# Where the even sums of down-projection pairs 2 to 11 are kept: weight-operand ring, or the two raw-weight tiles

## The chip, the cores and the metric

One core of one Trainium2 chip runs the whole program. The time is the device time of one execution in microseconds (us); of several executions the median is given. Engines are named as in the profile: PE multiplies matrices, PEld loads its weights, DVE and ACT are the vector and the scalar engine, POOL and SP are used here for moving data and for issuing DMAs.

## What is computed

Two layers of a small decoder, for 1024 prompt tokens and 8 sample tokens together (1032 columns, model width 1024). Layer 0 mixes tokens by a gated linear recurrence, layer 1 by windowed attention; each is followed by the same MLP, and only the MLP matters here:

```
def sq_relu_mlp(x, w_up, w_down):
    return jnp.square(jax.nn.relu(x @ w_up)) @ w_down
...
yp = yp + sq_relu_mlp(rms_norm(yp, norm_mlp_g[layer]), mlp_w_up[layer], mlp_w_down[layer])
```

`w_up` is 1024 x 4096 and `w_down` 4096 x 1024.

## The kernel before, in words

Activations lie transposed, features on the 128 partitions and 1032 columns. A matrix product is made in three passes: each operand is split into a rounded high part (ACT copy) and the low rest (DVE subtract), and PE adds high x high, high x low and low x high.

The two MLP projections are made in **pairs** of row blocks by a scheme of seven products in place of eight (2x2 blocks with sums and differences of blocks). `PROG` lists the products: 16 "up" pairs, then 20 "dn" (down) pairs, each with its products in the order 1, 2, 6, 7, 5, 4, 3. The first 14 of the 16 hidden pairs are handled so, in five chunks (`CHUNKS`: 3, 3, 3, 3 and 2 hidden pairs); four down pairs belong to each chunk, so down pairs 0 to 15 have 3 hidden pairs each and pairs 16 to 19 have 2. A product of the first kind is 3 x 3 x 2 = 18 matmuls of 258 columns, a pair 126. The rest of the hidden features follows at the end as an ordinary product (`down_steps`, matmuls of line 226).

Each down pair gathers two tiles of sums, the even one `he` and the odd one `ho` (128 x 1032). In order of the products: ACT copies product 1 from PSUM to `he` (line 633), DVE adds product 2 (635), ACT copies product 6 to `ho` and product 7 to the other half of `ho`, DVE adds to `ho` (637, 641), ACT copies product 3's sum to the other half of `he`. The four copies wait for PE, and PE waits for them: the third product goes on adding into the PSUM tile that the copy of the first one reads, the fifth into what the copy of the third reads. Then POOL adds `ho` and `he` to sums in DRAM by an accumulating DMA (line 652, "spill" in the profile); pairs 16 to 19 add from DRAM instead (654).

Tiles come from pools of fixed numbers of buffers, and an instruction that writes a new tile waits until the buffer's last user is done (for a stored tile: until its DMA has landed):

- `wp`, tag W, 12 buffers ("ring of weight operands"): the seven split weight operands `op` of a pair (lines 395 and 396: high and low in one tile), the two tiles `ws` of sums of weight blocks (line 497), and in down pairs 2 to 11 also `he`.
- `ap`, tag A, 33 buffers: activations, loaded hidden sums `tl` (line 542, POOL's DMA queue; split on ACT 401 and DVE 402), `ho`, and `he` of the other pairs.
- `rp`, tag R, 2 buffers: raw weights of the up pairs (fetched by SP, line 159), and the last four raw weight tiles of a layer (`last_weights`, line 604).
- tag Q, 4 buffers: raw weights of the down pairs, two tiles each (SP, line 159).

A list scheduler sets each engine's order of instructions; it knows the buffers, so a change of pools changes the order. Each engine, and SP's and POOL's DMA issuing too, then works strictly down its list: an instruction that waits holds up all that stand behind it. Operands are built some products ahead: after each product `pw.look(n)` lets the plan build up to a place in the next pair, as far as buffers are free.

Of the kernel before, what the change touches and what calls it, by code (L numbers as in the profile page):

```python
# [10 lines left out]
F32 = mybir.dt.float32  # L11
# [5 lines left out]
P = 128  # L17
D = 1024
M8 = D // P
SEQ = 1024  # L20
NS = 8
T = SEQ + NS
# [5 lines left out]
CHUNKS = [range(0, 3), range(3, 6), range(6, 9), range(9, 12), range(12, 14)]  # L28
# [31 lines left out]
def trunk(ctx: ExitStack, tc: tile.TileContext, I, O):  # L60
    nc = tc.nc
    pe, act, dve, pool, sp = nc.tensor, nc.scalar, nc.vector, nc.gpsimd, nc.sync

    cp = ctx.enter_context(tc.tile_pool(name="cp", bufs=1))
    ap = ctx.enter_context(tc.tile_pool(name="ap", bufs=33))
    wp = ctx.enter_context(tc.tile_pool(name="wp", bufs=12))
    rp = ctx.enter_context(tc.tile_pool(name="rp", bufs=2))
# [13 lines left out]
    def swap_small(name, bufs):  # L81
        open_small.close()
        small["pool"] = open_small.enter_context(tc.tile_pool(name=name, bufs=bufs, reuse_waits="tile"))
# [5 lines left out]
    def nm(s):  # L89
        cnt[0] += 1  # L90
        return f"{s}{cnt[0]}"

    def A(s="a"):
        return ap.tile([P, T], F32, tag="A", name=nm(s))
# [4 lines left out]
    def S(s="s"):  # L99
        return small["pool"].tile([P, CH], F32, tag="S", name=nm(s))  # L100
# [12 lines left out]
    def DB(tag):  # L113
        return psum["pool"].tile([P, 1024], F32, tag="D" + tag, bufs=2 if tag == "G" else 1, name=nm("bD"))

    def quarters(x):
        return x.rearrange("p (b c) -> p b c", b=2)

    def inner(d):
        return quarters(d)[:, :, 0:QT]  # L120
# [22 lines left out]
    def VV(n):  # L143
        o, w = VEC[n]
        return vec[:, o:o + w]
# [4 lines left out]
    raws = []  # L150

    def fetch(n):
        while len(raws) < min(n, len(units)):
            name, _, src, _ = units[len(raws)]
            if name[:2] == "dn":
                raws.append(small["pool"].tile([P, RQ], F32, tag="Q", name=nm("raw")))
            else:
                raws.append(rp.tile([P, D], F32, tag="R", name=nm("raw")))
            sp.dma_start(raws[-1][:, 0:src.shape[1]], src)

    def split_unit(raw, alloc, eng, parts=1):
# [209 lines left out]
    def factors(stat, ps):  # L371
        ssq, out = stat
        ssq.total(ps[:, :CH])
        rstd_m2(ps[:, :CH], out)
# [25 lines left out]
    def op_at(hi, lo):  # L400
        act.copy(r_(hi), lo)  # L401
        dve.tensor_tensor(r_(lo), lo, hi, ALU.subtract)  # L402
        return hi, lo
# [120 lines left out]
    def product(d, first, w, xs):  # L524
        n = len(xs)
        for j, (xh, xl) in enumerate(xs):
            for a, (wt, xt) in enumerate(((w[0], xh), (w[0], xl), (w[1], xh))):
                for b in range(2):
                    pe.matmul(d[:, 512 * b:512 * b + QT], lhsT=r_(wt[:, j * P:j * P + P]),  # L529
                              rhs=r_(xt[:, QT * b:QT * b + QT]),  # L530
                              start=first and j == 0 and a == 0, stop=j == n - 1 and a == 2,
                              skip_group_check=not first)
# [36 lines left out]
    def sums_of(e, o, to):  # L569
        t = small["pool"].tile([P, T], F32, tag="U", name=nm("ts"))  # L570

        def put(k, x):
            act.dma_start(to[:, k * HALF:k * HALF + x.shape[1]], x)

        put(2, o)
        yield
        dve.tensor_tensor(t[:, H0], e[:, H1], e[:, H0], ALU.subtract)
        dve.tensor_tensor(e[:, H1], o[:, H1], e[:, H1], ALU.subtract)
        dve.tensor_tensor(t[:, H1], o[:, H1], t[:, H0], ALU.subtract)
        yield  # L580
        put(0, e)
        put(4, t)
        dve.tensor_tensor(o[:, H0], o[:, H0], t[:, H1], ALU.subtract)
        yield
        put(6, o[:, H0])
# [3 lines left out]
    def mlp_products(layer, tok, pw, r, spill, acc, gnext, after):  # L589
        ahead = Ahead(layer)  # L590
        hs, raw = [], []
# [2 lines left out]
        xs[:] = [None] * M8  # L594
        st, stores = {}, []

        def last_tile(k):
            lo, hi = A("hdl"), A("hdh")
            pool.dma_start(lo, hid[layer][k])
            return hi, lo  # L600

        def last_weights(j):
            t = rp.tile([P, D], F32, tag="R", name=nm("raw"))
            sp.dma_start(t, I["w_dn"][layer][8 * len(CHUNKS) + j])
            return t

        for n, (kind, q, i) in enumerate(PROG):
            up = kind == "up"
            w, x = BY[i]
            if up and n in (1, 3, 5, 7, 9):  # L610
                tok.make(("B22", "T3", "T2", "T1", "T4")[n // 2])
            if n == 6:
                factors(rs.pop("late"), DB("Y"))
                swap_small(f"u{layer}", 3)
            if (kind, q, i) == ("up", NSP, 5):
                swap_small(f"q{layer}", 4)
            wt = pw.take(n)
            first = up and q < 2
            if i == 1:
                st[q] = {2: DB("X" if first and q == 1 else "Y"), "g": DB("G"),  # L620
                         "e": (W if not up and q in range(2, 12) else A)("he"), "o": A("ho")}
            z = st[q]
            alone = i in (1, 2, 7) or (i == 3 and first)
            if alone and i in (3, 7):
                z[i] = DB("Y" if first and q == 0 else "X")
            d = z["g"] if i in (1, 5, 6) else z[7] if i == 4 else z.get(i, z["g"])
            product(d, alone, wt, (tok if up else ahead).ops[x] if up else ahead.ops[q // 4][x])
            e, o, g = z["e"], z["o"], inner(z["g"])
            e0, e1, o0, o1 = [quarters(t[:, h]) for t in (e, o) for h in (H0, H1)]
            if i in (1, 6, 7, 3):  # L630
                t, f = {1: (e0, g), 6: (o0, g), 7: (o1, inner(d)), 3: (e1, inner(d))}[i]
                with tc.high_priority():
                    last["copy"] = act.copy(t, f).ins  # L633
            if i == 2:
                dve.tensor_tensor(e0, inner(d), e0, ALU.add)
            elif i == 5:
                dve.tensor_tensor(o1, g, o1, ALU.add)  # L637
                if 3 in z:
                    dve.tensor_tensor(e1, g, e1, ALU.add)
            elif i == 4:  # L640
                dve.tensor_tensor(o0, inner(d), o0, ALU.add)  # L641
            ready = {4: "o", 3: "" if alone else "e", 5: "e" if 3 in z else ""}.get(i, "")
            if ready and up:
                t = z[ready]
                dve.scalar_tensor_tensor(t, t, 0.0, r, ALU.min, ALU.mult)  # L645
                act.activation(t, t, AF.Square)  # L646
                if q >= NSP:
                    act.dma_start(hid[layer][2 * (q - NSP) + (ready == "o")], t)
            elif ready:
                m, t = 2 * (q % 4) + (ready == "o"), z[ready]  # L650
                if q < 4 * len(CHUNKS) - 4:
                    pool.dma_start(acc[m], t, accum_op=ALU.add)  # L652
                else:
                    pool.dma_start(t, acc[m], accum_op=ALU.add)
                    xs[m] = t
            if i == (4 if 3 in z else 3):
                if up and q < NSP:
                    stores.append(sums_of(e, o, hsum[layer][q]))
                del st[q]
            pw.look(n)  # L660
            for g in stores:
                next(g, None)
            if up and q == NPAIR - 1:
                k = ORDER.index(i)
                ahead.fetch(0, 3 * (k + 1), n)
                ahead.split(n)
            elif not up:
                c, k = q // 4, 7 * (q % 4) + ORDER.index(i)
                ahead.split(n)
                if c + 1 < len(CHUNKS):  # L670
                    ahead.fetch(c + 1, 11 * k // 20 if k <= 20 else 11 + 3 * (k - 20) // 2, n)
                k += 28 * (c - 3)
                if k in LAST["tile"]:
                    raw.append(last_tile(LAST["tile"].index(k)))
                if k in LAST["weights"]:
                    wraw.append(last_weights(LAST["weights"].index(k)))
                with tc.issue_after(last["copy"]):
                    if k in LAST["split tile"]:
                        hs.append(op_at(*raw.pop(0)))
                    if k in LAST["split weights"]:  # L680
                        ws.append(split_unit(wraw.pop(0), W, dve))
# [413 lines left out]


    sp8 = cp.tile([P, M8], F32, name="sp8")
    nsp8 = cp.tile([P, M8], F32, name="nsp8")
    lam = VV("lam")
    with_e = S("e")[:, :M8]  # L1100
    with_z = S("z")[:, :M8]
    act.activation(with_e, lam, AF.Abs)
# [276 lines left out]
```

## Time and profile before

| | us |
|---|---|
| median of 3 runs (2040.08 to 2043.04) | 2040.84 |
| the profiled execution's own time | 2038.14 |
| its span, first to last instruction | 2036.3 |
| PE busy | 2003.5 (98%) |
| DVE, ACT, POOL busy | 1413.2, 1051.9, 352.5 |
| mean granted TensorE clock | 0.996 |
| first to last matmul of the down pairs, layer 0 | 674 to 960 |
| the same, layer 1 | 1700 to 1988 |

The span is the profiler's; the time around it (1.8 us) belongs to start and end. PE is busy nearly throughout, so what counts is where PE stands still, and for whom. "Idle before" in the profile is the time an engine stood before an instruction, and the arrow names what ended it.

### The profile page before, as it was taken

Reading aid. Unit: us, or ns where it says so; the run is one execution under the profiler, and the core shown is the slowest. Engines: PE = TensorE matmul, PEld = TensorE weight load, DVE = VectorE, ACT = ScalarE, POOL = GpSimd, SP = SyncE. Lnnn points to the kernel's source line nnn. Section 1 sums busy time; section 2 is a strip of 40 time slices with the busy share of each in tenths; the row PEclk is TensorE's granted clock in tenths of the full one; section 3 lists DMA queues with packets and bytes.
Section 4 is the critical chain, followed back from the end, with each engine's and each line's share of the span. In section 5 each row is a group of like instructions: output and inputs, shape, how many; then the busy total and the mean of one; then the engine's idle time right before and its main releaser. Section 6 shows DMA issues by size and latency. Waiting matters only on the chain.

```text
span 2036.3 us, 38639 instructions
## 1 busy us (share of the span) xinstructions
PE 2003.5 (98%) x15106; PEld 1957.5 (96%) x15106; DVE 1413.2 (69%) x2673; ACT 1051.9 (52%) x2090; POOL 352.5 (17%) x562
## 2 busy tenths in 40 slices
PE   9989999999999999999999999999999999999999
PEld 8989999999999999999988887999999999999999
DVE  8887537876766766766846777569766666777663
ACT  6475635544343655555457776555434435555450
POOL 2541100000001223221003434100000003323220
PEclk9989999999999999999999999999999999999999
DMA  5112142344445777877443435612543447887683
GB/s 175 52 32 55 53 167 84 105 154 143 148 139 197 233 216 213 230 178 179 129 108 84 106 99 175 234 63 83 171 157 130 162 167 235 218 224 219 166 200 105
DMA packets 121047, 304.87 MB, mean 150 GB/s; under 512 B 20888, under 2 KB 53152, under 8 KB 120864
## 3 DMA queue, kind: packets, MB, share of 16 engines
q1 hardware_dynamic: 64864, 135.41, 21.6%
q0 software_dynamic: 28352, 98.30, 19.0%
q10 hardware_dynamic: 27648, 68.70, 9.3%
q8 instruction: 118, 1.93, 0.4%
q14 instruction: 65, 0.53, 0.1%
HBM read 176.22 MB, written 113.44 MB: 142 GB/s over the span
## 4 chain that ended last, share of the span: by engine, by line
PE 84%; issue 4%; DMA 3%; DVE 2%; ACT 2%; POOL 1%; SPq 0%; POOLq 0%; ACTq 0%
PE bD L529 54%; PE bP L226 11%; PE bS L226 6%; PE bP L768 4%; PE bT L226 3%; PE bO L889 2%; PE bS L848 1%; PE bT L868 1%; PE bN L714 1%; DMA spill<-ho 1%; DMA spill<-he 1%; DMA tl<-hsum 1%; PE bS L796 1%; POOL t L1170 0%; POOL tl L542 0%
## 5 line engine op out<-in xcount | busy, mean ns | idle before, releaser
L529 PE MATMUL bD<-op,op 128*128 128x258 f32 x5376 | 648.5, 283 | 0.0
L529 PEld LDWEIGHTS bD<-op,op 128*128 128x128 f32 x5376 | 647.9, 189 | 0.3
L529 PE MATMUL bD<-tl,op 128*128 128x258 f32 x4704 | 570.1, 284 | 4.4 <-ACT ho L633 4.1
L529 PEld LDWEIGHTS bD<-tl,op 128*128 128x128 f32 x4704 | 568.5, 190 | 5.8 <-ACT ho L633 4.5
L542 POOL DMA_DIRECT2D tl<-hsum x196 | 115.5, 674 | 900.2 <-ACT ho L633 421.6
L396 DVE TENSOR_TENSOR op<-ws,op 128x512 fp32r<-128x512 f32 (+2 forms) x288 | 168.5, 598 | 84.2 <-ACT op L395 84.2
L633 ACT COPY ho<-bD 128x516 f32<-128x516 f32 x144 | 85.1, 591 | 226.8 <-PE bD L529 226.8
L402 DVE TENSOR_TENSOR tl<-tl 128x516 fp32r<-128x516 f32 x196 | 130.6, 692 | 93.5 <-ACT tl L401 89.8
L395 ACT CAST op<-ws 128x512 fp32r<-128x512 f32 (+2 forms) x288 | 153.4, 550 | 42.0 <-DVE op L396 23.4
L633 ACT COPY he<-bD 128x516 f32<-128x516 f32 x144 | 84.0, 583 | 167.6 <-PE bD L529 167.6
L396 DVE TENSOR_TENSOR op<-raw,op 128x512 fp32r<-128x512 f32 (+2 forms) x216 | 124.1, 597 | 62.6 <-ACT op L395 62.6
L395 ACT CAST op<-raw 128x512 fp32r<-128x512 f32 (+2 forms) x216 | 114.1, 549 | 43.6 <-PE bD L529 20.3
L401 ACT CAST tl<-tl 128x516 fp32r<-128x516 f32 x196 | 115.3, 627 | 3.5 <-DMA tl<-hsum 3.5
L646 ACT ACTIVATE ho<-ho 128x1032 f32<-128x1032 f32 x32 | 34.2, 1070 | 107.5 <-DVE ho L645 107.5
L166 DVE TENSOR_TENSOR wl<-raw,wh 128x1024 fp32r<-128x1024 f32 (+1 forms) x57 | 68.1, 1201 | 25.1 <-ACT wh L165 20.3
L641 DVE TENSOR_TENSOR ho<-bD,ho 128x516 f32<-128x516 f32 x72 | 49.9, 694 | 43.3 <-PE bD L529 43.3
L859 POOL TENSOR_SCALAR se<-se,den 128x256 f32<-128x256 f32 (+1 forms) x128 | 66.4, 524 | 76.3 <-DVE den L857 74.3
L165 ACT CAST wh<-raw 128x1024 fp32r<-128x1024 f32 (+1 forms) x60 | 58.6, 988 | 37.1 <-DMA raw<-w_in 15.3
L652 POOL DMA_DIRECT2D spill<-ho x32 | 28.7, 896 | 257.2 <-DVE ho L641 245.9
L852 DVE CUSTOM_DVE_ANT_0 se<-bS,bias,nsink 128x256 f32<-128x256 f32 (+1 forms) x128 | 56.4, 461 | 21.6 <-PE bS L848 16.8
L855 ACT ACTIVATE se<-se,den 128x257 f32<-128x257 f32 (+1 forms) x128 | 63.0, 496 | 14.8 <-DVE den L852 13.2
L637 DVE TENSOR_TENSOR ho<-bD,ho 128x516 f32<-128x516 f32 x72 | 49.8, 691 | 20.2 <-PE bD L529 13.1
(299 smaller groups left out, 3743.6 us busy)
## 6 DMA issues: line engine op xcount, KB each, us to landing
tl<-hsum POOLq DMA_DIRECT2D x196, 258.0 KB, 7.2
raw<-w_up SPq DMA_DIRECT2D x64, 512.0 KB, 3.7
raw<-w_dn SPq DMA_DIRECT2D x64, 384.0 KB, 6.6
spill<-ho POOLq DMA_DIRECT2D x32, 516.0 KB, 5.6
spill<-he POOLq DMA_DIRECT2D x32, 516.0 KB, 7.2
hsum<-ho ACTq DMA_DIRECT2D x28, 516.0 KB, 3.7
hsum<-he ACTq DMA_DIRECT2D x28, 516.0 KB, 2.7
hsum<-ts ACTq DMA_DIRECT2D x28, 516.0 KB, 3.4
```

The source lines that it names most:

```text
L166: eng.tensor_tensor(r_(lo[:, sl]), raw[:, sl], hi[:, sl], ALU.subtract)
L226: pe.matmul(o, lhsT=r_(wt[:, col(k):col(k) + P]), rhs=r_(xt[:, cs(c)]), start=(k == first and a == 0), stop=(k == final and a == 2))
L395: act.copy(r_(t[:, 0:n]), src)
L396: dve.tensor_tensor(r_(t[:, n:2 * n]), src, t[:, 0:n], ALU.subtract)
L401: act.copy(r_(hi), lo)
L402: dve.tensor_tensor(r_(lo), lo, hi, ALU.subtract)
L529: pe.matmul(d[:, 512 * b:512 * b + QT], lhsT=r_(wt[:, j * P:j * P + P]), rhs=r_(xt[:, QT * b:QT * b + QT]), start=first and j == 0 and a = ...
L542: pool.dma_start(t[:, n:2 * n], src)
L633: last["copy"] = act.copy(t, f).ins
L768: pe.matmul(ps[c], lhsT=r_(wt[:, k * P:k * P + P]), rhs=r_(xt[:, cs(c)]), start=(k == 0 and a == 0), stop=(k == M8 - 1 and a == 2))
L855: act.activation(se[:, u, 256 - n:257], se[:, u, 256 - n:257], AF.Exp, scale=-1.0, bias=dn[:, u:u + 1], accum_out=dn[:, 2 + u:3 + u])
L859: pool.tensor_scalar(e, e, dn[:, 2 + u:3 + u], 0.0, ALU.mult, ALU.add)
```

## The change

`he` of down pairs 2 to 11 is taken from the two R tiles, by the new helper `spare`, and no longer from ring W. For that the R tiles grow from 1024 to 1032 columns; the room is made by writing the small vector `nsp8` over the `lam` columns of `vec`, which nothing reads after it.

```
-                raws.append(rp.tile([P, D], F32, tag="R", name=nm("raw")))
+                raws.append(rp.tile([P, T], F32, tag="R", name=nm("raw")))
...
+        def spare(s):
+            return rp.tile([P, T], F32, tag="R", name=nm(s))
...
-            t = rp.tile([P, D], F32, tag="R", name=nm("raw"))
-            sp.dma_start(t, I["w_dn"][layer][8 * len(CHUNKS) + j])
+            t = rp.tile([P, T], F32, tag="R", name=nm("raw"))
+            sp.dma_start(t[:, 0:D], I["w_dn"][layer][8 * len(CHUNKS) + j])
...
-                         "e": (W if not up and q in range(2, 12) else A)("he"), "o": A("ho")}
+                         "e": spare("he") if not up and q in range(2, 12) else A("he"), "o": A("ho")}
...
-    nsp8 = cp.tile([P, M8], F32, name="nsp8")
-    lam = VV("lam")
+    lam = nsp8 = VV("lam")
```

No instruction is added or taken away. The orders of PE and of POOL stay the same in the whole program; those of ACT, DVE and SP differ, in the down pairs of both layers alike (and nowhere else, but for the name of `nsp8`).

On ACT, before, the stretch of layer 0 from the first copy of pair 11 (`he1025`) on. `op` are split weight operands, `raw` and `ws` what they are split from; the block of seven holds the last five operands of pair 11 itself and the first two of pair 12:

```order
L633 COPY he1025_9281<-bD1024_9280 128x516
L395 CAST op1028_9304<-ws1021_9272 128x384
L395 CAST op1029_9308<-raw996_9031 128x384
L395 CAST op1031_9332<-ws1027_9302 128x384
L401 CAST tl1015_9197<-tl1015_9197 128x516
L395 CAST op1034_9360<-ws1021_9272 128x384
L395 CAST op1037_9385<-ws1027_9302 128x384
L395 CAST op1042_9417<-raw997_9033 128x384
L395 CAST op1044_9444<-raw1016_9218 128x384
L633 COPY ho1026_9282<-bD1024_9280 128x516
L633 COPY ho1026_9282<-bD1036_9365 128x516
```

And now, from the same copy on (the four operands belong to pair 12):

```order
L636 COPY he1025_9280<-bD1024_9279 128x516
L401 CAST tl1015_9196<-tl1015_9196 128x516
L395 CAST op1055_9510<-raw1016_9217 128x384
L395 CAST op1056_9534<-ws1053_9504 128x384
L636 COPY ho1026_9281<-bD1024_9279 128x516
L395 CAST op1057_9560<-ws1047_9472 128x384
L395 CAST op1060_9587<-ws1053_9504 128x384
L636 COPY ho1026_9281<-bD1036_9364 128x516
L401 CAST tl1020_9249<-tl1020_9249 128x516
```

The seven operands that stood in one block behind a pair's first copy are spread over the pair, one to three behind each copy, and they are those of a pair later. Before, the operand of a pair's third product stood behind the copy of that same pair's first product; now it stands some ten products ahead of its use.

On SP, before, the first two loads of last weights (line 604) stand at the beginning of the layer's down weights, right behind the up weights, since the two R tiles are free there:

```order
L159 DMA raw750_6818<-w_up 128x1024
L604 DMA raw1095_9892<-w_dn 128x1024
L159 DMA raw751_6820<-w_dn 128x768
L159 DMA raw778_7059<-w_dn 128x768
L159 DMA raw779_7061<-w_dn 128x768
L159 DMA raw780_7063<-w_dn 128x768
L604 DMA raw1098_9920<-w_dn 128x1024
```

Now they stand behind the 29th and the 31st load of the layer's down weights (`raw1041` belongs to pair 14, `raw1061` too, `raw1062` and `raw1081` to pair 15), since the R tiles are those of `he` of pairs 10 and 11 until their stores have landed:

```order
L159 DMA raw1041_9414<-w_dn 128x768
L607 DMA raw1095_9891<-w_dn 128x1024
L159 DMA raw1061_9613<-w_dn 128x768
L159 DMA raw1062_9615<-w_dn 128x768
L607 DMA raw1098_9919<-w_dn 128x1024
L159 DMA raw1081_9798<-w_dn 128x768
```

What moved there is these two loads, past 29 and 27 others; what stands behind them in SP's list now waits with them.

## The prediction

> **What bounds the kernel now.** I begin with the page: which engine is busy, and before which instructions it stood.
>
> ```profile
> span 2036.3 us, 38639 instructions
> ...
> PE 2003.5 (98%) x15106; PEld 1957.5 (96%) x15106; DVE 1413.2 (69%) x2673; ACT 1051.9 (52%) x2090; POOL 352.5 (17%) x562
> ...
> L529 PE MATMUL bD<-tl,op 128*128 128x258 f32 x4704 | 570.1, 284 | 4.4 <-ACT ho L633 4.1
> ```
>
> PE is the bound at 98%, so no change outside PE's own work can bring more than the time in which PE stands or runs slowly. In the down products (`tl` by `op`) it stood 4.4 us in both layers together. The waits of PE name the cause by number of times:
>
> ```profile
> PE bD L529 <- ACT ho L633: 4.1, 2, 2.1
> ...
> PE bD L529 <- DVE ho L637: 0.3, 1, 0.3
> ```
>
> Two waits make nearly all of it, and the timeline of PE shows one in each layer:
>
> ```profile
> 867.36 2.91 PE L529 MATMUL bD<-tl,op 128*128 128x258 f32 x22 [1.96 <-ACT ho L633]
> ...
> 1893.39 2.83 PE L529 MATMUL bD<-tl,op 128*128 128x258 f32 x14 [2.12 <-ACT ho L633]
> ```
>
> Why was ACT late with its copy of `ho`? Its own timeline at these two places, in order of start, length and instruction:
>
> ```profile
> 861.33 0.51 ACT L395 CAST op<-ws 128x384 fp32r<-128x384 f32 x1
> 865.89 0.51 ACT L395 CAST op<-raw 128x384 fp32r<-128x384 f32 x1 [4.06 <-DMA spill<-he]
> 866.31 0.51 ACT L395 CAST op<-ws 128x384 fp32r<-128x384 f32 x1
> 866.72 0.58 ACT L633 COPY ho<-bD 128x516 f32<-128x516 f32 x1
> ...
> 1891.92 0.51 ACT L395 CAST op<-raw 128x384 fp32r<-128x384 f32 x1 [4.52 <-DMA spill<-he]
> 1892.34 0.51 ACT L395 CAST op<-ws 128x384 fp32r<-128x384 f32 x1
> 1892.76 0.58 ACT L633 COPY ho<-bD 128x516 f32<-128x516 f32 x1
> ```
>
> An operand of pair 13 waits 4.06 and 4.52 us until the store of an even sum has landed: that sum held the W buffer which the operand is to fill. The copy on which PE depends stands two instructions behind it. POOL's timeline tells which sums those are, those of pairs 10 and 11, the last ones in ring W:
>
> ```profile
> 842.92 0.89 POOL L652 DMA_DIRECT2D spill<-he  x1 [2.27 <-ACT tl L401]
> ...
> 858.62 0.88 POOL L652 DMA_DIRECT2D spill<-he  x1 [1.07 <-ACT he L633]
> ```
>
> The store of pair 10 delays DVE, too: its timeline has a wait of 1.51 us for the same reason, and the sum `ho` for which PE stood 0.3 us comes behind it.
>
> ```profile
> 850.29 0.56 DVE L497 TENSOR_TENSOR ws<-raw,raw 128x384 f32<-128x384 f32 x1 [1.51 <-DMA spill<-he]
> ...
> 853.51 0.69 DVE L637 TENSOR_TENSOR ho<-bD,ho 128x516 f32<-128x516 f32 x1
> ```
>
> **What the stalls cost in PE's time.** An idle time is not the whole price, so I count matmuls. The chain of waits gives their pace where nothing stops them, 484.70 / 4020 = 0.1206 us; 18 of them, one product, are 2.17 us, and a pair of 126 is 15.2 us.
>
> ```profile
> 367.08 484.70 PE bD L529 x4020
> ```
>
> The down products in stretches of 15 us (busy time, matmuls, granted clock, DMA share, GB/s):
>
> ```profile
> 830.00:845.00 15.00, 15.00 (x127) 1.00 0.69 171
> 845.00:860.00 15.00, 14.68 (x122) 1.00 1.01 327
> 860.00:875.00 15.00, 13.04 (x108) 1.00 0.58 165
> ...
> 890.00:905.00 15.00, 15.00 (x127) 1.00 0.64 156
> ...
> 1885.00:1900.00 15.00, 12.88 (x95) 0.89 0.58 168
> ```
>
> Against 127, layer 0 lacks 5 + 19 = 24 matmuls, 2.9 us; layer 1 lacks 32, 3.9 us. Layer 1's stall is hardly longer, but its clock is lower. In steps of 1 us:
>
> ```profile
> 1894.00:1895.00 1.00, 1.00 (x8) 0.55 0.82 280
> 1895.00:1896.00 1.00, 1.00 (x6) 0.50 0.29 114
> 1896.00:1897.00 1.00, 1.00 (x7) 0.50 0.00 0
> 1897.00:1898.00 1.00, 1.00 (x9) 0.75 0.00 0
> ```
>
> Behind its 2.12 us of idle time the granted clock fell to 0.50 and needed until 1898 to come back: 30 matmuls in 4 us against 44 in four stretches of eleven, so 14 x 0.1206 = 1.7 us. Behind layer 0's 1.96 us it stayed at 1.00. So a stall here costs 2.2 to 2.9 us, and 1.7 us more if the clock falls.
>
> [...]
>
> **The change, part by part.**
>
> (1) *Even sums out of ring W.* No instruction is added or removed, and no duration changes by the place of a tile as far as rows show. What goes is the wait of `op` and `ws` for a store. All 12 W buffers then serve operands, which come free by PE's own progress. I take the whole loss: 2.9 + 3.9 = **6.8 us**; bounds are the two idle times and the DVE wait alone, 1.96 + 2.12 + 0.3 = 4.4, and 6.8 + 1.7 = 8.5 if in other executions the clock falls in layer 0 as well. I settle on 6.6, a little under the count, since 127 in 15 us is partly matmuls that overlap a window's edge.
>
> (2) *The new order on ACT and DVE.* Operands stand one to three behind each copy, some ten products ahead of use, where before the tightest stood two ahead. Each needs the buffer of a product which PE ends no later than the one copied just before, so it should wait little. The trace of before contains this order already, in pairs 12 to 14, where no sum is in W: the stretch 890 to 905 above holds 127 matmuls at no loss, and ACT's waits there for an operand's buffer are small.
>
> ```profile
> ACT op L395 <- PE bD L529: 0.2, 1, 0.2
> ```
>
> So I take nothing for it; from both sides, 0.2 us in each of some ten pairs and two layers would be 4 us of ACT's time, hidden as long as a copy (0.59 us) ends within the 2.17 us of the product between.
>
> (3) *A ring of two for the even sums.* A new wait: the first copy of pair q+2 must find the store of pair q landed. Behind that copy on ACT stand the next operands and the copy of `ho`; PE needs it at the third product of q+2, that is nine products or 19.5 us after the end of pair q, less 0.59 for the copy. The sum's last half is copied and its DMA issued about 1.5 us after the end of the pair, and accumulating DMAs land so (least, median, longest of all down pairs of layer 0):
>
> ```profile
> DMA to landing us min/median/max: 5.3/6.5/11.0
> ```
>
> 1.5 + 11.0 = 12.5, so 6.4 us remain even with the longest. I take 0; a store would have to need 17.4 us to cost anything.
>
> (4) *Last weights later on SP.* The two loads stand before the 30th and the 32nd of the down loads. Before, those were fetched in the second of these rows; the second last-weight load was issued 220 us earlier, in the first:
>
> ```profile
> 644.55 0.38 SPq L604 DMA_DIRECT2D raw<-w_dn  x1
> ...
> 861.38 5.98 SPq L159 DMA_DIRECT2D raw<-w_dn  x2
> ```
>
> Now the second waits for the store of pair 11 (858.62 + 7.20 by the chain, so 865.8), and the last weights of pair 15 behind it are issued at about 866.5. Landing takes
>
> ```profile
> DMA to landing us min/median/max: 2.9/6.6/7.5
> ```
>
> so they are there by 874. ACT splits them behind the fourth product of pair 13, eleven products or 23.9 us after the end of pair 11, which is at about 857 (1.5 us before POOL's 858.62): 881. Seven us remain; and a late operand there first holds up ACT alone, not PE. The last weights themselves are split later still. I take 0; the price is what traffic does (rival below).
>
> (5) *`nsp8` over `lam`, R tiles 8 columns wider:* one 128 x 8 write goes elsewhere, in the same order; 0.
>
> **Sum:** 2038.14 - 6.6 = 2031.5 for an execution with profile, whose span would be about 2029.7. The runs shown lie higher than the profiled execution by 2.70 at the median, so **2040.84 - 6.6 = 2034.2 us**. Forecast's own range: 2032.3 (8.5) to 2035.2 (5.6).
>
> **Rivals.**
>
> *The clock does not fall behind such stalls in the timed runs.* Then the gain is the stalls' own, 2.9 in layer 0 and 3.9 - 1.7 = 2.2 in layer 1, about 5.1: 2035.7 us. For it: one fall in two stalls of nearly one length. Against: it did fall once, behind 2.12 us. [...]
>
> *Traffic takes the place of the store.* The two loads of 512 KB moved from 644 to 850 and 866, where the DMA engines are full (share, GB/s):
>
> ```profile
> 851.00:853.00 2.00, 1.00 1.03 402
> ...
> 871.00:873.00 2.00, 1.00 0.00 0
> ```
>
> 1.05 MB at 402 GB/s is 2.6 us in a stretch in which ACT already waited for a loaded tile:
>
> ```profile
> ACT tl L401 <- DMA tl<-hsum: 0.3, 1, 0.3
> ```
>
> If ACT is late by 2.6 + 0.3, less the 1.6 us of slack of a copy (2.17 - 0.59), PE loses 1.3 us in each layer and, with one fall of the clock, 4.3 in all: the gain is 2.3, 2038.5 us. Against it: right behind, from 871 on, the engines are idle, and operands are farther ahead.
>
> *It doesn't do what it says:* operands wait for raw weights, not for a buffer, and the wait stays: 2040.8. Against: the rows above name the store, in both layers.
>
> *Slower: two tiles are too few.* If stores land later than 17.4 us, the first copy of pairs 4 to 11 waits, eight times in each layer, on the engine that PE waits for. At 0.7 us a time that is 11.2, less 6.6: 2045.4 us. For it: the new order makes bursts of loads and accumulating stores fall differently, and the share is above 1 for 20 us on end. Against: the longest landing was 11.0.
>
> **How the numbers follow.** Forecast 0.60, no fall of the clock 0.14, traffic 0.14, no effect 0.04, two tiles too few 0.08. A measurement of this kernel can tell about 0.2%, 4.1 us, from no change: under 2036.8 is faster, over 2044.9 slower. Faster: 0.60 + 0.14 + a little of traffic, 0.75; within 0.2%: 0.17; slower: 0.08. The range reaches from 2032.3, the forecast's end, to 2038.8, past the traffic case; left out are no effect, too few tiles and the edges, under 0.2.
>
> **What would show it.** Right: in PE's waits the line `ho` L633 at 4.1 us gone or under 1; no wait of ACT's operands or DVE's `ws` for a store of `he`; the stretches at 845, 860 and 1885 at 126 or 127 matmuls with clock 1.00. Wrong in (3): ACT's `he` L633 waits for spill. Wrong in (4): an operand from raw weights, or a `tl`, waits for a DMA between 850 and 885. Wrong as a whole: PE's idle time before the down products still above 3 us.

## The result, and the profile after

The changed kernel takes 2032.92 us (median of 8 executions, 2031.05 to 2037.18), the kernel before 2040.46 (8 executions, 2036.54 to 2043.23). The ratio is 0.9965, 95% interval 0.9956 to 0.9974, that is 7.1 us less, 5.3 to 9.0. Forecast were 6.6 us less and 2034.2 us.

The page's first rows, and the row of the down products, on the changed kernel:

```profile
span 2032.2 us, 38742 instructions
...
PE 2001.2 (98%) x15106; PEld 1956.2 (96%) x15106; DVE 1413.9 (70%) x2673; ACT 1056.3 (52%) x2090; POOL 352.8 (17%) x562
...
L529 PE MATMUL bD<-tl,op 128*128 128x258 f32 x4704 | 567.7, 283 | 0.0
```

The counts by engine are those of before; the 103 instructions more are of kinds that this row doesn't count. The idle time before the down products is 0.0, where it was 4.4, and the waits of PE no longer name them. The three stretches of 15 us that lacked matmuls are full, at full clock:

```profile
845.00:860.00 15.00, 15.00 (x127) 1.00 1.04 323
860.00:875.00 15.00, 15.00 (x127) 1.00 0.84 217
1885.00:1900.00 15.00, 15.00 (x128) 1.00 0.86 219
```

The best measure of the MLP's paired products is one layer's 4896 matmuls from the second row of the chain to the first matmul of line 226. After, the chain of waits has each layer in one unbroken piece:

```profile
368.22 590.42 PE bD L529 x4896
...
1393.28 590.23 PE bD L529 x4896
```

Before, the same two stretches began at 367.08 (shown with the prediction) and 1394.03, and ended where line 226 begins:

```profile
960.46 13.28 PE bP L226 x84
...
1394.03 6.00 PE bD L529 x48
...
1987.96 7.13 PE bP L226 x45
```

960.46 - 367.08 = 593.38 and 1987.96 - 1394.03 = 593.93, so layer 0 won 2.96 us and layer 1 3.70, together 6.66. The profiled execution as a whole fell by 2038.14 - 2033.93 = 4.2 only: the products of layer 0 began 1.14 us later and 1.07 were lost between the two layers' products, parts whose instructions and order the change doesn't touch. Two more executions of the kernel before (below) began these products at 366.37 and 366.38, so such shifts come and go.

The place of the stall, ACT after. The split of the operand at 861.35 is, by its place in pair 12 and by what it reads, the counterpart of the one that waited 4.06 us (the rows carry no buffer numbers):

```profile
859.29 0.59 ACT L636 COPY he<-bD 128x516 f32<-128x516 f32 x1
859.78 1.67 ACT L401 CAST tl<-tl 128x516 fp32r<-128x516 f32 x3
861.35 0.51 ACT L395 CAST op<-raw 128x384 fp32r<-128x384 f32 x1
861.77 0.51 ACT L395 CAST op<-ws 128x384 fp32r<-128x384 f32 x1
863.60 0.59 ACT L636 COPY ho<-bD 128x516 f32<-128x516 f32 x1 [1.32 <-PE bD L529]
```

It waits for nothing, and now it is the copy of `ho` that waits for PE. The store of pair 11 is still in flight at that time: POOL issued it at 858.02 and it landed 8.6 us later (9.0 us in layer 1), which is later than the 7.20 of before. SP's second load of last weights, which needs it landed, goes out at 866.84.

```profile
850.68 0.33 SPq L607 DMA_DIRECT2D raw<-w_dn  x1
851.10 6.50 SPq L159 DMA_DIRECT2D raw<-w_dn  x2
866.84 0.33 SPq L607 DMA_DIRECT2D raw<-w_dn  x1
867.26 9.82 SPq L159 DMA_DIRECT2D raw<-w_dn  x3
```

### The profile page after: what moved, and what is told of

Read it like the earlier page. It is cut to its first block, busy times and chain, and to the rows that moved or that the text cites. A ratio compares the mean times of both kernels' runs of the same rounds, so it can differ in the third digit from the quotient of the medians.

```text
span 2032.2 us, 38742 instructions
## 1 busy us (share of the span) xinstructions
PE 2001.2 (98%) x15106; PEld 1956.2 (96%) x15106; DVE 1413.9 (70%) x2673; ACT 1056.3 (52%) x2090; POOL 352.8 (17%) x562
## 4 chain that ended last, share of the span: by engine, by line
PE 89%; DVE 2%; ACT 2%; issue 1%; POOL 1%; DMA 1%; SPq 0%; ACTq 0%; POOLq 0%
PE bD L529 60%; PE bP L226 11%; PE bS L226 6%; PE bP L771 4%; PE bT L226 3%; PE bO L892 1%; PE bS L851 1%; PE bT L871 1%; PE bN L717 1%; POOL t L1172 1%; PE bS L799 1%; POOL ri L1173 0%; DVE wl L166 0%; DVE xc L1135 0%; DMA od0l<-o 0%
```

## The experiments

All numbers of a layer below are from the chain of the run's one profile, as above; "over" means over the changed kernel's 590.42 and 590.23. The ratio is of whole executions (eleven of each experiment, six of "two more sums in W", eight of the change itself). The kernel before, timed beside the experiments, took 2039.71 us at the median for the four from "only 10 and 11 moved" to "two more sums in W", and 2037.14 us for the last two, which ran on another chip. One profile need not be a typical execution: those of "only 10 and 11 moved" and of "stores in halves" were the fastest of their eleven, that of "layout only" the slowest. So layers and ratio can differ by some us.

| run | layers 0 and 1, us | over, us | PE idle for copies | ratio to before, 95% |
|---|---|---|---|---|
| before, first profile | 593.38, 593.93 | 2.96, 3.70 | 1.96, 2.12 | |
| before, second | 593.55, 593.15 | 3.13, 2.92 | 2.48, 2.48 | |
| before, third | 593.78, 595.19 | 3.36, 4.96 | 2.69, 2.38 | |
| all changed | 590.42, 590.23 | 0, 0 | 0, 0 | 0.9965, 0.9956 to 0.9974 |
| only 10 and 11 moved | 591.66, 591.53 | 1.24, 1.30 | 0.9, 1.3 | 0.9988, 0.9979 to 0.9997 |
| only 2 to 9 moved | 593.55, 591.81 | 3.13, 1.58 | 2.4, 1.2 | 1.0003, 0.9994 to 1.0011 |
| layout only | 595.02, 593.89 | 4.60, 3.66 | 2.4, 2.1 | 0.9991, 0.9982 to 1.0 |
| two more sums in W | 590.73, 590.11 | 0.31, -0.12 | 0, 0 | 0.9975, 0.9964 to 0.9987 |
| no early operands | 592.01, 592.03 | 1.59, 1.80 | 0, 0 | 0.9987, 0.9978 to 0.9996 |
| stores in halves | 593.04, 591.02 | 2.62, 0.79 | 2.2, 0.7 | 1.0004, 0.9995 to 1.0013 |

The first theory was that the stores of pairs 10 and 11 land late, because a burst of loads begins in pair 11, and hold W buffers meanwhile. Its rivals: the last sum in W stops an operand wherever it is, since the scheduler puts that operand too early; or operands spread over the pair help everywhere.

**Only pairs 10 and 11 moved.**

```
-  "e": spare("he") if not up and q in range(2, 12) else A("he")
+  "e": (spare if not up and q in (10, 11) else W if not up and q in range(2, 10) else A)("he")
```

> Only the even sums of pairs 10 and 11 lie in the raw-weight tiles; those of pairs 2 to 9 stay in ring W. The operand that meets the last sum in W is now one of pair 11, behind the store of pair 9, away from the burst of loads that begins in pair 11. Theory (what cost was the stores of pairs 10 and 11 landing late, in full traffic, while they hold W buffers): the store of pair 9 lands in 5 to 6.5 us, ACT waits at most 2.5 us there, PE stands under 0.6 us per layer; the 4896 matmuls of a layer's products take 590.2 to 591.2 us (before 593.4 and 593.9), and the time is 5 to 6.6 us under before. Rival (the last sum in W always stops its operand, wherever it is, because the scheduler puts the operand too early): PE stands 2 us in each layer at pair 10, and the gain is under 2.5 us. Rival (the operands spread out in all pairs are what helps): the gain is about a quarter, 1.5 us.

ACT's and POOL's timelines at pair 10 of layer 0 (first row POOL, the store of pair 9), and PE's:

```profile
825.39 0.89 POOL L655 DMA_DIRECT2D spill<-he  x1 [0.71 <-ACT he L636]
...
832.57 0.52 ACT L395 CAST op<-raw 128x384 fp32r<-128x384 f32 x1 [4.38 <-DMA spill<-he]
832.99 0.51 ACT L395 CAST op<-ws 128x384 fp32r<-128x384 f32 x1
833.40 0.58 ACT L636 COPY ho<-bD 128x516 f32<-128x516 f32 x1
...
834.03 4.25 PE L529 MATMUL bD<-tl,op 128*128 128x258 f32 x33 [0.89 <-ACT ho L636]
```

The same kind of wait two pairs earlier: 4.38 us for the store of pair 9, and PE stood 0.89 us (1.3 in layer 1). The theory had asked for under 0.6 us and a gain of 5 or more; measured are 2.4 us, 0.6 to 4.3, so it fell as it was put. What it took for granted didn't come about, though: pair 9's store, which landed in 6.5 us in the first profile of before, took 7.1 us here (7.5 in layer 1), so this run doesn't say that the landing has no part. The rival with the early operand was right in kind and high in size.

The size of a stall follows from two times. PE ran out of work 6.8 us after the issue of pair 11's store in layer 0 of before, 7.6 in layer 1, and 7.7 after that of pair 9's store here; and it went on about 1.5 us after the landing (865.8 and 867.36 in layer 0 of before). Landing plus 1.5 less the first time gives the stalls: 7.2 + 1.5 - 6.8 = 1.9 and 8.2 + 1.5 - 7.6 = 2.1 before (measured 1.96 and 2.12), 7.1 + 1.5 - 7.7 = 0.9 and 7.5 + 1.5 - 7.7 = 1.3 here (0.89 and 1.34). In layer 0 most of the difference comes from the issue: here the store left 1.3 us ahead of the next pair's first copy (826.66), before 0.6 ahead (858.62 and 859.26). In layer 1 it comes from the landing.

**Only pairs 2 to 9 moved.** The same line with 10 and 11 exchanged for 2 to 9.

> The opposite part: pairs 2 to 9 in the raw-weight tiles, pairs 10 and 11 in ring W as before. Theory: the two waits of about 2 us stay where they were, the layers take 593 to 594 us, the gain is 0 to 1.5 us. Rival (spread operands in all pairs): about three quarters of the gain, 5 us.

```profile
866.09 0.51 ACT L395 CAST op<-raw 128x384 fp32r<-128x384 f32 x1 [4.50 <-DMA spill<-he]
```

The wait is where it was before, 4.50 us for the store of pair 11, and the time is that of before (ratio 1.0003). Layer 1 missed the expectation: pair 11's store landed there in 7.3 us, PE stood 1.2 us only, and the layer took 591.81 where 593 to 594 was asked for. Operands spread over eight of ten pairs bring nothing that the time shows; that rival falls.

**Layout only.** Wider R tiles and `nsp8` over `lam`, all sums in W.

```
-  "e": spare("he") if not up and q in range(2, 12) else A("he")
+  "e": (W if not up and q in range(2, 12) else A)("he")
```

> The raw-weight tiles 8 columns wider and the small vector written over lam, but all even sums of pairs 2 to 11 in ring W as before. Theory and rivals alike: the time of before, within 2 us; layers of 593 to 594 us. A difference would mean that the place of tiles in memory matters by itself.

PE stood 2.4 and 2.1 us, and the time is 1.8 us below before, 0 to 3.7: at the edge of what can be told, and the layers are not shorter. The place in memory does not take the stall away.

**Two more sums in W.** In the kernel before:

```
-  (W if not up and q in range(2, 12) else A)("he")
+  (W if not up and q in range(2, 14) else A)("he")
```

> The kernel before with two more even sums, those of pairs 12 and 13, in ring W. Theory (landing in traffic is what cost): the last sum in W is now that of pair 13, whose store falls into a stretch where the DMA engines are half idle; it lands in 5 to 6.5 us, PE stands under 0.6 us per layer, and the time is 4 to 6.6 us under before, though W is used more. Rival (ring W is too short for operands and sums, so the fewer sums in it the better): same as before or slower, by 0 to 3 us. Rival (the last sum in W always stops its operand): the waits of 2 us move by two pairs, and the gain is 0 to 2 us.

Ring W is used more, and the stall is gone: 5.1 us under before, 2.7 to 7.3. ACT at pair 14, the first pair whose sum is not in W:

```profile
887.95 0.59 ACT L633 COPY he<-bD 128x516 f32<-128x516 f32 x1 [1.04 <-PE bD L529]
888.44 0.63 ACT L401 CAST tl<-tl 128x516 fp32r<-128x516 f32 x1
892.29 0.59 ACT L633 COPY ho<-bD 128x516 f32<-128x516 f32 x1 [3.23 <-PE bD L529]
```

The time is what the first theory had forecast, but not for its reason: no operand stands between the two copies here, so none can wait for the store of pair 13. In pair 14 of before and of the changed kernel none stands there either; from there on the splits of the last weights take W buffers, which may be why, but this wasn't tried. That too many sums in W cause this stall is refuted.

So a second theory: where the use of ring W changes, the scheduler puts an operand early, into the buffer of the last sum in W and ahead of a copy that PE needs, as if that store landed sooner than in 7 us (no run shows what landing time the scheduler reckons with). Two runs to test it.

**No early operands.** The kernel before, sums in W as they were, only the order changed:

```
-  pw.look(n)
+  if not up and q >= 12:
+      with tc.issue_after(last["copy"]):
+          pw.look(n)
+  else:
+      pw.look(n)
```

> The kernel before, its even sums in ring W as before, but the operands looked ahead for from pair 12 on are held behind the latest copy in ACT's and DVE's lists, so that the block of operands stays behind a pair's first copy through to the end and none is put early behind the last sum in W. Theory as the first runs left it (where the use of ring W changes, the scheduler puts an operand early, into the buffer of the last sum in W and ahead of a copy that PE needs; the store takes some 7 us to land): no operand waits for a store of he, PE stands under 0.5 us in the down pairs of each layer, a layer's 4896 matmuls take 590.2 to 591.5 us, the time is 4 to 6.6 us under before. Rival (the sums themselves, holding buffers while their stores land, starve PE): the waits stay, 593 us a layer, and the gain is under 1 us.

ACT has no wait for a store of `he` any more. At pair 12 the operands between its first copy and that of `ho` start at once, and the copy waits for PE:

```profile
857.06 0.59 ACT L633 COPY he<-bD 128x516 f32<-128x516 f32 x1 [0.54 <-PE bD L529]
857.55 0.52 ACT L395 CAST op<-ws 128x384 fp32r<-128x384 f32 x1
857.96 0.51 ACT L395 CAST op<-raw 128x384 fp32r<-128x384 f32 x1
...
861.42 0.59 ACT L633 COPY ho<-bD 128x516 f32<-128x516 f32 x1 [0.95 <-PE bD L529]
```

Yet in layer 0 the store of pair 11 landed no sooner than before, in 7.3 us (6.7 in layer 1, where it was 8.2). The stretches of 15 us show where time is still lost:

```profile
845.00:860.00 15.00, 14.79 (x122) 1.00 1.05 319
860.00:875.00 15.00, 15.00 (x127) 1.00 0.62 153
...
920.00:935.00 15.00, 14.50 (x118) 1.00 0.88 184
```

860 to 875, where 19 matmuls were lacking, is full. Left are the sum `ho` behind DVE's wait for the store of pair 10 (845; PE stood 0.2 us; in layer 1 it is the store of pair 2, and 0.7 us), and a new loss in pair 16 of each layer (118 where the changed kernel has 123), in which an operand held back now comes 0.5 us late. So the layers end at 592.0, outside the 591.5 asked for, and the gain is 2.7 us, 0.8 to 4.5. The stall itself goes with the order alone, while sums stay in W: the second theory holds for its cause. The smaller loss, by DVE's wait, does come from sums in W.

**Stores in halves.** Pairs 10 and 11 store the first half of `he` right after its last add:

```
+  if not up and q in (10, 11):
+      pool.dma_start(acc[2 * (q % 4)][:, H0], e[:, H0], accum_op=ALU.add)
...
+  if q in (10, 11) and ready == "e":
+      pool.dma_start(acc[m][:, H1], t[:, H1], accum_op=ALU.add)
-  if q < 4 * len(CHUNKS) - 4:
+  elif q < 4 * len(CHUNKS) - 4:
```

> The kernel before, order and buffers untouched, but the even sums of pairs 10 and 11 are stored in two halves: the first half as soon as its last add is done (after the pair's second product), the second at the end, so that only 258 KB are left to land at the end in place of 516. Theory: the last store lands in 3.5 to 5 us in place of 7.2, ACT's wait of 4.1 and 4.5 us shrinks to 0.5 to 2, PE stands under 0.5 us, layers of 590.3 to 591.5 us, 4 to 6.6 us under before. Rival (it is not the landing but the buffer or the order): waits and time as before, within 1.5 us.

```profile
856.80 0.88 POOL L654 DMA_DIRECT2D spill<-he  x1 [1.06 <-ACT he L633]
...
865.24 0.51 ACT L395 CAST op<-raw 128x384 fp32r<-128x384 f32 x1 [4.64 <-DMA spill<-he]
...
1889.80 0.51 ACT L395 CAST op<-raw 128x384 fp32r<-128x384 f32 x1 [3.10 <-DMA spill<-he]
```

In layer 0 the half of 258 KB needed 8.3 us to land, longer than the whole 516 KB before (7.20), and the wait stayed. In layer 1 it needed 6.7 us where the whole had needed 8.2; ACT waited 3.10 us, PE stood 0.7, and the layer took 591.02, inside what was asked for. Expected were 3.5 to 5 us in both: half the size does not halve the landing here. The DMA engines were full at that time (share 1.04 to 1.07 from 855 to 863, 1.04 to 1.08 in the kernel before); whether that is why the half took so long was not tried by itself. The time is that of before (ratio 1.0004). Where the landing did get shorter, in layer 1, the stall shrank with it, as the sum of two times above wants (6.7 + 1.5 - 7.6 = 0.6). So, as far as these runs show, the early operand makes the stall, and the landing sets its size.

**Before, twice more, for the clock.**

> The kernel before once more, for the clock alone. Theory: PE stands 1.9 to 2.6 us in each layer behind the store of pair 11, as in the first profile; whether the granted clock then falls to 0.50 for about 3 us varies between layers and executions; where it falls, the layer takes 1.3 to 1.9 us longer. [...]

> As the run above: two more stalls of 1.9 to 2.6 us, with or without a fall of the clock; over the four stalls of the two runs the theory wants at least one fall and at least one without.

PE's timeline and its stretches of 1 us in the third profile of before, layer 0 first:

```profile
867.06 3.15 PE L529 MATMUL bD<-tl,op 128*128 128x258 f32 x24 [2.69 <-ACT ho L633]
...
1896.38 3.82 PE L529 MATMUL bD<-tl,op 128*128 128x258 f32 x17 [2.38 <-ACT ho L633]
```

```profile
868.00:869.00 1.00, 1.00 (x11) 1.00 0.82 295
...
1897.00:1898.00 1.00, 1.00 (x6) 0.50 0.86 323
1898.00:1899.00 1.00, 1.00 (x7) 0.50 0.18 71
1899.00:1900.00 1.00, 1.00 (x7) 0.57 0.00 0
```

Behind the longer stall the clock stayed, behind the shorter one it fell. In the second profile it stayed behind both (2.48 us each). One fall in these four stalls is what the theory wanted; the stall of 2.69 us is a little longer than it gave. The layout-only run had a fall in each layer, behind these:

```profile
866.11 4.24 PE L529 MATMUL bD<-tl,op 128*128 128x258 f32 x23 [2.41 <-ACT ho L636]
...
1897.08 3.29 PE L529 MATMUL bD<-tl,op 128*128 128x258 f32 x18 [2.07 <-ACT ho L636]
```

## Why the prediction was right, point by point

**The stall and its cause.** Both stalls and DVE's wait are gone, by the path that was forecast: the operand's split at 861.35 does not wait. The runs sharpen it. It is not that sums in W are too many (two more of them do no harm) nor that the last two are special (with them alone moved, pair 9's takes their part). The wait arises where the last sum leaves W and the scheduler at once puts an operand into its buffer, and its size goes by how late the store lands. The prediction's listing of orders held the fact but didn't say this: the spread order in pairs 12 to 14 of before was taken as a proof of its harmlessness, and it is harmless only past its beginning. The stretch it showed for this, 890 to 905, is pair 14, in which ACT's timeline has no operand before 903.96; the row of 0.2 us beside it is from 885 to 900, and its one wait is in pair 13 (884.97). Pair 13 does have the spread order, and lost nothing either (127 matmuls from 875 to 890).

**The sizes.** Term (1) was 6.6 with ends 4.4 and 8.5. The profile measured 6.66. Over three profiles of before the layers cost 6.66, 6.05 and 8.32 us more than after, 7.0 on the mean, and the timed difference is 7.1. That 6.66 meets 6.6 so closely is partly luck: the three profiles differ by up to 2.3 us, by how late a store lands and whether the clock falls. The idle times alone, 4.4, would have been short: 2.2 to 2.9 us of lost matmuls for each stall, and the clock on top, were needed. The price of a fall, 1.7, was somewhat high (1.5 below): in windows of 1 us a matmul that crosses an edge counts twice, so that four of them hold 44 where the pace of 0.1206 us gives 33.

**Terms taken as nothing.** (2) ACT's waits of operands for PE grew from 4.8 to 11.0 us in layer 0's down pairs, about half a us each, with PE at 127 matmuls a stretch: nothing. (3) Stores of layer 0, pairs 1 to 15:

```profile
DMA to landing us min/median/max: 5.3/7.1/8.7
```

far under 17.4 (layer 1: 10.0 at most), and no copy of `he` waited for a store. One new wait was not foreseen: in layer 1 a copy of `ho` waited 2.3 us for a store of an `ho`; PE did not stand for it. (4) The second load of last weights went out at 866.84 where 866.5 was forecast, the weights of pair 15 right behind it at 867.26; ACT waited for no raw weights. (5) is borne out by the layout-only run as far as it can tell.

**The rivals.** The clock does fall, but not behind every stall: of the ten stalls of 1.96 us or more in the three profiles of before, the layout-only run and those with 2 to 9 moved and with half stores, it fell behind four, of 2.07, 2.12, 2.38 and 2.41 us, and stayed at 1.00 behind the longest, 2.69, and the shortest, 1.96. The price is 94.6 - 93.1 = 1.5 us (the 768 matmuls behind the stall, with and without a fall). No run here shows what decides whether it falls. So "no fall in the timed runs" was too simple, and so was a fixed one per execution. Traffic: ACT's wait for loaded tiles is 1.4 us in layer 0's down pairs, 1.6 before; nothing was given back. Two tiles too few: refuted by (3).

**What was off:** the profiled execution, 2033.93 for 2031.5, by 2.4 us that other parts of the program took more in it, 1.14 + 1.07 of them in the two places named above.

## What to carry to other kernels

A buffer that is held until a DMA has landed stops whoever the scheduler puts into it next, here ACT for 4.06 and 4.52 us behind stores that landed in 7.20 and 8.2; look in the engine's list at what stands between that instruction and the next one on which the busiest engine waits. A place to look at first is where tiles cease to use a ring, for there the order can change at once; it cost PE time here behind pair 9 (0.89 and 1.34 us) and pair 11 (1.96 to 2.69 us in the kernel before), and not behind pair 13. Price such a stall by missing matmuls in fixed stretches and not by the idle time before one instruction (2.9 and 3.9 us here, where the two idle times were 1.96 and 2.12), and take the length of the stage, not of the whole run, as the measure when the gain is a third of a per cent.

## What the runs showed of the hardware that was not expected

The clock granted to TensorE fell to 0.50 for about 3 us behind idle times of 2.07 to 2.41 us, in four of ten stalls, without an order by length. And half of an accumulating store, 258 KB, took 8.3 us to land in layer 0, with the DMA engines full (share 1.04 to 1.07 from 855 to 863), and 6.7 in layer 1, where the whole of 516 KB took 7.20 and 8.2: half the size brought no sure gain.
